# Low weight parts by accumulating DMA in a hybrid decoder layer (four gate/up blocks and all of down)

## The chip, the cores and the metric

The kernel runs on one core of one Trainium2 chip. The metric is the device time of one execution in microseconds (us). The engines named below are PE (matrix multiply; PEld is its weight load), ACT (ScalarE), DVE (VectorE), POOL (GpSimd) and SP (SyncE, which here only issues DMAs). Each engine works through its own queue in order; semaphores tie the queues together.

## What is computed

One decoder layer on 512 tokens of width 1024: a mixer with eight attention heads and eight gated groups, a projection back, a layer norm, then a SwiGLU feed-forward part with 2816 hidden units and a second layer norm.

```
merged = concat(rms_norm(attention(x @ w_q, x @ w_k, x @ w_v)), rms_norm(spatial_gating(gelu(x @ w_u), gelu(x @ w_z))))
x = layer_norm(alpha * x + merged @ w_out)             # "LN1" below
ffn = (silu(x @ w_gate) * (x @ w_up)) @ w_down
x = layer_norm(alpha * x + ffn)                        # "LN2"
```

All data are float32. The inputs weigh 58 MB as the chip reads them, nearly all of it weights.

## The kernel before, in words

**Split products.** PE multiplies in a float32 form that keeps fewer bits (F32R). To keep the accuracy, each operand is split into a high part (the operand rounded to F32R) and a low part (operand minus high part), and each product is three matmuls: high by high, high by low, low by high (`mm3`, and `product` in the gate/up stage). So every weight tile of 128 x 1024 (512 KB), after its load, needs a high copy and a low part. `split` (lines 232 to 241) makes them: the high copy on ACT (line 238), or on DVE for three tiles (line 236), and the low part by a subtraction (line 239) on DVE, or on POOL where the caller says so (`far`).

**Buffers.** The class `W` (line 251) holds a weight tile of q, k, z, u, out and down: the raw load `wr` rotates through 2 buffers, the high part `wh` and the low part `wl` through 3 each. A new tile can be split only when PE has finished with the tile three before it. Two early users have buffers of their own: the first four gate/up blocks (pairs 0 and 1; high parts `pth` and `ptl`, low parts `znh` and `znl`), and the last four tiles of down (`qk`, `qk`, `zg`, `ug`).

**Stages.** In the order of time: V and QK projections, attention mixed with the gated part, output projection of both halves, LN1 with its transposes, gate/up, down, LN2. Out-projection and LN1 go by four token tiles t = 0 to 3 of 128 tokens: two PSUM banks for each t (one for each half of the columns), then `layer_norm` (line 679): an add per half (line 750) that needs a reciprocal root `ra[t]` made on POOL (line 275, `pow`), statistics (687, 688), another pow on POOL, normalisation (700 on ACT or 696 and 707 on DVE), gain (702), bias (711; for t = 1 on POOL), then PE transposes (760) and the splits into operands of gate/up (`V`, `qk`, `xh`, `ug`).

**Gate/up.** Eleven pairs of hidden tiles; each pair takes seven block products instead of eight by a Strassen-like scheme, whose extra blocks are sums that DVE makes in PSUM (line 933). A block is 24 matmuls of 256 columns. For pairs 0 and 1 the first two blocks are prepared early, by `whole` (line 826), while out-projection and LN1 run.

**Down.** `down_w(f)` (line 963) loads and splits tile f of w_down and splits the hidden activations of that tile (ACT line 973, DVE line 974); `down_mm` multiplies for four token tiles and two halves, 24 matmuls of 512 columns a tile. 22 tiles; the last six are finished token tile by token tile, so that LN2 of a token tile runs beside the products of the next.

**What sets the order.** Every operation is recorded with an engine, a cost in us and the buffers that it reads and writes (`op`). `plan` (line 107) is a list scheduler: it simulates the engines with these costs, takes on each engine the ready operation of the lowest rank, and so fixes the order of every queue. The costs that concern the change are MM (one `mm3` on 512 columns), the cost of a DMA on SP and its latency DMA_LAT. A cost that is changed can move instructions on any engine, also far from the code it belongs to.

Of the kernel before, what the change touches and what calls it, by code (L numbers as in the profile page):

```python
# [8 lines left out]
AF = mybir.ActivationFunctionType  # L9
# [22 lines left out]

SAME, CROSS, DMA_LAT, MM, MM256 = 0.15, 0.19, 1.9, 0.643, 0.36
SEQ = ('q1', 'a1', 'q0', 'z', 'q2', 'a0', 'u', 'q3', 's', 'a2', 'a3')
# [27 lines left out]
class Order:  # L62
# [13 lines left out]

    def op(self, eng, cost, fn, r=(), w=(), base=None, table=None, lock=False):
        o = Op()
        o.eng, o.cost, o.fn, o.table, o.lock = eng, cost, fn, table, lock
        o.lat = DMA_LAT if eng == "SP" else 0.0  # L80
        o.prio = (self.base if base is None else base, len(self.ops))
# [104 lines left out]
def build(tc, cp, wp, ap, ps, xt, xtok, w_vqk, w_zu, w_out, w_gu, w_dn, wsp, cst, rows, cols, out):  # L186
# [5 lines left out]
    def act(n, fn, r, w, aps=0, acc=False, **k):  # L192
        od.op("ACT", 0.075 + 0.000833 * n + 0.093 * (aps + acc), fn, r, w, **k)
# [7 lines left out]
    def dma(kb, fn, r, w, **k):  # L201
        od.op("SP", max(0.46, kb / 352.0), fn, r, w, **k)
# [31 lines left out]
    def split(n, src, hi, lo, rs, ws_hi, ws_lo, far=False, lock=True, near=False, **k):  # L234
        if near:
            dve(n, lambda: V.tensor_scalar(hi(), src(), 1.0, None, op0=ALU.mult), rs, ws_hi, per=0.52, lock=True, **k)
        else:
# [3 lines left out]
               lock=lock, **k)  # L241

    def mm3(cost, o, lh, ll, rh, rl, start, stop, r, w, **k):
        def fn():
            PE.matmul(o(), lhsT=lh(), rhs=rh(), start=start, stop=False)  # L245
            PE.matmul(o(), lhsT=lh(), rhs=rl(), start=False, stop=False)  # L246
            PE.matmul(o(), lhsT=ll(), rhs=rh(), start=False, stop=stop)  # L247

        pe(cost, fn, r, w, **k)

    class W:


        def __init__(self, src, tag=None, mid=None, group=None):
# [12 lines left out]
            if mid is not None:  # L267
                mid(raw)
            split(WCH, lambda: raw.t, lambda: self.hi(every), lambda: self.lo(every), [raw], hk, lk, group in WPOOL,
                  near=group in WHI, base=RANK["w"])  # L270
# [525 lines left out]
    class Raw:  # L796


        def __init__(self, p, j, slot):
# [3 lines left out]
            else:  # L803
                self.t, self.key = (lambda c=slice(0, WCH): zgr.t[:, slot, c]), (zgr, slot)
            dma(512, lambda: nc.sync.dma_start(self.t(), w_gu[4 * p + j]), [], [self.key], base=PREP)

# [19 lines left out]
    def whole(raw, early=None):  # L826
        return Blk(early).fill(raw.t, raw.key, far=early in EPOOL)

# [78 lines left out]
    pairs = [Pair(p) for p in range(NP)]  # L907
    EARLY, EPOOL = 2, (0, 1, 2, 3)
    first = [[Raw(0, 0, "wr"), Raw(0, 3, "wr")], [Raw(1, 0, 0), Raw(1, 3, 1)]]
# [53 lines left out]
    def down_w(f, tag=None):  # L963
        w = W(w_dn[f], tag)
        if f < FT - 4:
# [112 lines left out]
```

## Time and profile before

| | us |
|---|---|
| three runs | 570.74, 571.74, 1094.83 |
| median of them | 571.74 |
| the profiled execution, its own time | 570.17 |
| its span in the trace | 568.1 |
| PE busy | 547.5 (96%) |
| DVE busy | 413.2 (73%) |
| ACT busy | 280.9 (49%) |
| POOL busy | 157.0 (28%) |
| DMA engines busy (queue q1) | 34.6% of 16 engines' span |

A busy PE is read with care: its instructions are pipelined, and an instruction that runs at half the clock counts as busy too. Besides the totals, these views are used: the windows (busy time of each engine and the granted clock of PE in a stretch), the waits (who waited for whom), the chain that ended last, and the timeline (instructions in order of time; the number in brackets behind a row is the idle time ahead of it and what ended it). A line number can be that of a helper: 239 stands for all subtractions of `split`.

### The profile page before, as it was taken

Reading aid. Unit: us, or ns where it says so; the run is one execution under the profiler, and the core shown is the slowest. Engines: PE = TensorE matmul, PEld = TensorE weight load, DVE = VectorE, ACT = ScalarE, POOL = GpSimd, SP = SyncE. Lnnn points to the kernel's source line nnn. Section 1 sums busy time; section 2 is a strip of 40 time slices with the busy share of each in tenths; the row PEclk is TensorE's granted clock in tenths of the full one; section 3 lists DMA queues with packets and bytes.
Section 4 is the critical chain, followed back from the end, with each engine's and each line's share of the span. In section 5 each row is a group of like instructions: output and inputs, shape, how many; then the busy total and the mean of one; then the engine's idle time right before and its main releaser. Section 6 shows DMA issues by size and latency. Waiting matters only on the chain.

```text
span 568.1 us, 8774 instructions
## 1 busy us (share of the span) xinstructions
PE 547.5 (96%) x3360; PEld 488.6 (86%) x3360; DVE 413.2 (73%) x707; ACT 280.9 (49%) x482; POOL 157.0 (28%) x119
## 2 busy tenths in 40 slices
PE   9999999999899968999999999999999999999994
PEld 5888888887688857999999999999999888888883
DVE  5537779879975699998788788888877723334385
ACT  6323796788864347544545544544455422323211
POOL 0026258613205730253333242343322200000011
PEclk9999999999999979899999999999999999999998
DMA  7745514155715201432332333333124332232311
GB/s 260 265 131 153 140 48 129 43 163 182 226 38 194 102 3 72 144 127 103 112 112 76 115 109 109 116 111 112 38 75 149 112 111 94 92 112 74 112 74 74
DMA packets 21225, 65.51 MB, mean 115 GB/s; under 512 B 2880, under 2 KB 3392, under 8 KB 21184
## 3 DMA queue, kind: packets, MB, share of 16 engines
q1 hardware_dynamic: 21184, 64.96, 34.6%
q8 instruction: 26, 0.43, 0.3%
q14 instruction: 15, 0.12, 0.1%
HBM read 58.66 MB, written 2.10 MB: 107 GB/s over the span
## 4 chain that ended last, share of the span: by engine, by line
PE 94%; DVE 2%; ACT 2%; issue 0%; POOL 0%; DVEq 0%
PE pj L838 22%; PE sc L838 17%; PE pj L245 12%; PE pj L247 12%; PE pj L246 12%; PE sc L245 2%; PE sc L247 2%; PE sc L246 2%; PE pv L481 2%; PE tp L464 1%; PE sc L426 1%; PE pv L247 1%; PE pv L245 1%; PE tp L247 1%; PE tp L245 1%; PE tp L246 1%
## 5 line engine op out<-in xcount | busy, mean ns | idle before, releaser
L239 DVE TENSOR_TENSOR wl<-wr,wh 128x1024 fp32r<-128x1024 f32 (+1 forms) x55 | 71.8, 1306 | 60.7 <-ACT wh L238 60.1
L238 ACT ACTIVATE wh<-wr 128x1024 fp32r<-128x1024 f32 (+1 forms) x58 | 57.8, 999 | 84.4 <-PE sc L247 54.0
L838 PE MATMUL pj<-qk,wh 128*128 128x256 f32 x352 | 65.6, 287 | 1.2 <-ACT wh L238 1.2
L838 PE MATMUL sc<-xh,wh 128*128 128x256 f32 x352 | 64.5, 284 | 0.0
L838 PEld LDWEIGHTS pj<-qk,wh 128*128 128x128 f32 x352 | 55.8, 195 | 1.4 <-ACT wh L238 1.4
L838 PEld LDWEIGHTS sc<-xh,wh 128*128 128x128 f32 x352 | 55.1, 193 | 0.0
L275 POOL TENSOR_TENSOR sm<-sm,only 128x1 f32<-128x1 f32 (+1 forms) x20 | 16.4, 825 | 137.8 <-DVE sm L274 137.7
L838 PE MATMUL pj<-V,wh 128*128 128x256 f32 x288 | 52.6, 283 | 0.0
L838 PE MATMUL pj<-qk,wl 128*128 128x256 f32 x176 | 50.7, 288 | 0.4 <-DVE wl L239 0.4
L838 PE MATMUL sc<-xh,wl 128*128 128x256 f32 x176 | 49.8, 283 | 0.0
L245 PE MATMUL pj<-wh,xh 128*128 128x512 f32 x114 | 46.3, 406 | 0.0
L838 PEld LDWEIGHTS pj<-V,wh 128*128 128x128 f32 x288 | 44.9, 192 | 0.0
L246 PE MATMUL pj<-wl,xh 128*128 128x512 f32 x114 | 44.6, 391 | 0.0
L838 PE MATMUL pj<-V,wl 128*128 128x256 f32 x144 | 40.8, 283 | 0.0
L247 PE MATMUL pj<-wh,xl 128*128 128x512 f32 x96 | 37.7, 393 | 0.0
L239 POOL TENSOR_TENSOR wl<-wr,wh 128x1024 fp32r<-128x1024 f32 x7 | 17.2, 2456 | 72.8 <-ACT wh L238 67.9
L838 PEld LDWEIGHTS pj<-qk,wl 128*128 128x128 f32 x176 | 34.3, 195 | 0.8 <-DVE wl L239 0.8
L838 PEld LDWEIGHTS sc<-xh,wl 128*128 128x128 f32 x176 | 33.9, 192 | 0.0
L238 ACT ACTIVATE wh<-tp 128x512 fp32r<-128x512 f32 x33 | 19.7, 596 | 27.9 <-PE sc L838 26.0
L838 PE MATMUL sc<-ug,wh 128*128 128x256 f32 x176 | 32.1, 283 | 0.0
L239 DVE TENSOR_TENSOR wl<-tp,wh 128x512 fp32r<-128x512 f32 x33 | 22.6, 684 | 8.6 <-ACT wh L238 8.6
L245 PE MATMUL pj<-wh,pr 128*128 128x512 f32 x72 | 28.0, 389 | 0.0
(331 smaller groups left out, 1512.1 us busy)
## 6 DMA issues: line engine op xcount, KB each, us to landing
wr<-w_dn SPq DMA_DIRECT2D x22, 512.0 KB, 3.2
zg<-w_gu SPq DMA_DIRECT2D x16, 512.0 KB, 3.4
wr<-w_gu SPq DMA_DIRECT2D x16, 512.0 KB, 3.5
kl<-w_gu SPq DMA_DIRECT2D x14, 512.0 KB, 3.3
wr<-w_vqk SPq DMA_DIRECT2D x8, 512.0 KB, 3.6
wr<-w_zu SPq DMA_DIRECT2D x8, 512.0 KB, 3.3
wr<-w_out SPq DMA_DIRECT2D x8, 512.0 KB, 4.1
wr<-w_vqk SPq DMA_DIRECT2D x8, 256.0 KB, 4.0
```

Source lines behind the costliest of these rows:

```text
L238: act(n, lambda: A.activation(hi(), src(), AF.Copy), rs, ws_hi, **k)
L239: either("P" if far else "D", n, lambda E: E.tensor_tensor(out=lo(), in0=src(), in1=hi().bitcast(F32), op=ALU.subtract), [*rs, *ws_hi], ws_lo,
L245: PE.matmul(o(), lhsT=lh(), rhs=rh(), start=start, stop=False)
L246: PE.matmul(o(), lhsT=lh(), rhs=rl(), start=False, stop=False)
L247: PE.matmul(o(), lhsT=ll(), rhs=rh(), start=False, stop=stop)
L275: od.op("POOL", 0.3 + 0.165 * n, lambda: PL.tensor_tensor(out=o.t, in0=v.t, in1=mhalf.t[:, :n], op=ALU.pow), [v, mhalf], [o], lock=True)
L426: PE.matmul(sc.t[:, :n], lhsT=qs.t[:, e, ts], rhs=ks.t[:, 2 * e + 1, :n], start=False, stop=True)
L464: PE.transpose(tp.t[:, j * P:j * P + P], p.t[:, j * P:j * P + P], ident.t)
L481: PE.matmul(pv.t[:, j * P:], lhsT=vs.t[:, j, h, :], rhs=pt.t[:, j * S:j * S + w], start=j == 0 and i == 0, stop=j == NT - 1 and i == 1)
L838: PE.matmul(o, lhsT=lh(w), rhs=buf.t[:, s + rh, x], start=first and side == k == i == 0, stop=k == 3 and i == 2, skip_group_check=True)
```

## The change

The low parts of the first four gate/up blocks and of all 22 tiles of down are no longer made by subtraction. ACT writes the high part, and then writes the tile with its sign turned, rounded to F32R, into the low part's place: that is minus the high part. Then a DMA issued from POOL's queue adds the weights once more from DRAM onto it, so that the operand minus the high part stands there. The raw tile is read by the two ACT copies alone. In the planner, one `mm3` costs 0.681 instead of 0.643, and an accumulating DMA takes POOL 1.0 and lands 4.0 later.

```
-SAME, CROSS, DMA_LAT, MM, MM256 = 0.15, 0.19, 1.9, 0.643, 0.36
+SAME, CROSS, DMA_LAT, MM, MM256 = 0.15, 0.19, 1.9, 0.681, 0.36
+GROW, GROW_LAT = 1.0, 4.0
...
-        o.lat = DMA_LAT if eng == "SP" else 0.0
+        o.lat = DMA_LAT if eng == "SP" else lat
...
+    def split_dram(n, src, dram, hi, lo, rs, ws_hi, ws_lo, **k):
+
+        act(n, lambda: A.activation(hi(), src(), AF.Copy), rs, ws_hi, **k)
+        act(n, lambda: A.activation(lo(), src(), AF.Copy, scale=-1.0), rs, ws_lo, **k)
+        od.op("POOL", GROW, lambda: nc.gpsimd.dma_start(lo(), dram, accum_op=ALU.add), ws_lo, ws_lo, lat=GROW_LAT, **k)
...
+            if group == "down":
+                split_dram(WCH, lambda: raw.t, src, lambda: self.hi(every), lambda: self.lo(every), [raw], hk, lk,
+                           base=RANK["w"])
+                return
...
     def whole(raw, early=None):
-        return Blk(early).fill(raw.t, raw.key, far=early in EPOOL)
+        if early is None:
+            return Blk(early).fill(raw.t, raw.key)
+        b, c = Blk(early), slice(0, WCH)
+        split_dram(WCH, raw.t, raw.src, lambda: b.hi(c), lambda: b.lo(c), [raw.key], [b.hk], [b.lk], base=PREP)
+        return b
...
-    EARLY, EPOOL = 2, (0, 1, 2, 3)
+    EARLY = 2
...
-        w = W(w_dn[f], tag)
+        w = W(w_dn[f], tag, group="down")
```

In the changed kernel the line numbers are 10 to 16 higher. Over the whole program DVE issues 22 instructions fewer, ACT 26 more, and POOL loses 4 subtractions and gets 26 DMAs; PE and SP issue the same instructions. Their order differs in many places before gate/up, hardly within gate/up, and little behind it.

**Place 1: POOL at the end of out-projection.** `sm` at L275 (L286 in the changed kernel) are the pow operations; the four in a row give `ra[t]`, the next ones the root of LN1's variance for t = 0 and t = 1; the rows on `znl` and `znh` are the low parts of the four early blocks. Before:

```order
L239 TENSOR_TENSOR znl_1997<-zg_1951,ptl_1986 128x1024
L239 TENSOR_TENSOR znl_1997<-zg_1951,ptl_2020 128x1024
L239 TENSOR_TENSOR znh_2049<-wr_1999,pth_2031 128x1024
L275 TENSOR_TENSOR sm_2077<-sm_2055,only_7_73 128x1
L275 TENSOR_TENSOR sm_2082<-sm_2060,only_7_73 128x1
L275 TENSOR_TENSOR sm_2088<-sm_2062,only_7_73 128x1
L275 TENSOR_TENSOR sm_2091<-sm_2064,only_7_73 128x1
L239 TENSOR_TENSOR znh_2049<-wr_2033,pth_2069 128x1024
L275 TENSOR_TENSOR sm_2125<-sm_2118,only_7_73 128x1
L275 TENSOR_TENSOR sm_2171<-sm_2160,only_7_73 128x1
```

Three of the four subtractions stand ahead of the first pow. In the changed kernel the same place reads:

```order
L286 TENSOR_TENSOR sm_2026<-sm_2018,only_7_73 128x1
L286 TENSOR_TENSOR sm_2034<-sm_2020,only_7_73 128x1
L286 TENSOR_TENSOR sm_2045<-sm_2022,only_7_73 128x1
L286 TENSOR_TENSOR sm_2051<-sm_2024,only_7_73 128x1
L248 DMA znl_2029<-w_gu 128x1024 x2
L248 DMA znh_2065<-w_gu 128x1024
L286 TENSOR_TENSOR sm_2102<-sm_2097,only_7_73 128x1
L248 DMA znh_2065<-w_gu 128x1024
L286 TENSOR_TENSOR sm_2123<-sm_2117,only_7_73 128x1
```

The four pows have moved ahead of everything that concerns the early blocks, and three of the accumulating DMAs stand ahead of the pow of t = 0, the fourth ahead of that of t = 1.

**Place 2: PE at the end of out-projection.** `tp` and `pv` at L760 (L771) are the transposes of a token tile's two halves, `pj_2114` is a bank of token tile 3, `pj_2227` the first early block's product. Before:

```order
L247 MATMUL pj_2107<-ug_2004,xh_1526 128x512
L245 MATMUL pj_2114<-ug_2004,xh_1526 128x512
L246 MATMUL pj_2114<-ug_2004,xh_1526 128x512
L247 MATMUL pj_2114<-ug_2004,xh_1526 128x512
L760 MATMUL tp_2155<-only_1_206,xl_1510 128x128 x4
L760 MATMUL pv_2164<-only_1_206,xl_1510 128x128 x4
L760 MATMUL tp_2197<-only_1_206,xl_1510 128x128 x4
L760 MATMUL pv_2213<-only_1_206,xl_1510 128x128 x4
L838 MATMUL pj_2227<-V_2174,pth_2031 128x256 x2
```

All of token tile 3's matmuls precede the transposes of t = 0 and t = 1. In the changed kernel, where `pj_2134` and `pj_2147` are token tile 3's banks:

```order
L254 MATMUL sc_2089<-ug_1997,xh_1516 128x512
L252 MATMUL pj_2134<-wh_1921,xh_1516 128x512
L253 MATMUL pj_2134<-wl_1930,xh_1516 128x512
L254 MATMUL pj_2134<-wh_1921,xh_1516 128x512
L771 MATMUL tp_2139<-only_1_206,xl_1555 128x128 x4
L252 MATMUL pj_2147<-wh_1921,xh_1516 128x512
L253 MATMUL pj_2147<-wl_1930,xh_1516 128x512
L254 MATMUL pj_2147<-wh_1921,xh_1516 128x512
L771 MATMUL pv_2153<-only_1_206,xl_1555 128x128 x4
L252 MATMUL pj_2134<-wh_1932,xh_1516 128x512
```

The transposes of t = 0 have moved 21 and 18 matmuls forward, into token tile 3's product. What these rows don't show: the banks of t = 0 are also finished sooner. Between the last matmul of its second bank and the first one of token tile 3 stand 18 matmuls of 512 columns before and 33 after the change, while the place of token tile 3's first matmul in PE's queue is the same.

**Place 3: ACT and POOL where gate/up ends.** `wh_4915` (`wh_4919`) is the high part of down's first tile, `pr` at L882 (L898) the silu of the last hidden tiles, `xh` and `pr` at L973 (L989) the splits of activations. ACT before:

```order
L238 ACTIVATE wh_4886<-wr_4506 128x1024
L238 ACTIVATE wh_4915<-wr_4813 128x1024
L882 ACTIVATE pr_4917<-pr_4917 128x256
L973 ACTIVATE xh_4950<-znh_4410 128x512
L973 ACTIVATE pr_4958<-atr_2366 128x512
L238 ACTIVATE wh_4963<-wr_4913 128x1024
```

and in the changed kernel:

```order
L239 ACTIVATE wh_4890<-wr_4510 128x1024
L246 ACTIVATE wh_4919<-wr_4817 128x1024
L898 ACTIVATE pr_4921<-pr_4921 128x256
L247 ACTIVATE wl_4933<-wr_4817 128x1024
L989 ACTIVATE pr_4945<-atr_2391 128x512
L989 ACTIVATE xh_4953<-znh_4414 128x512 x2
L246 ACTIVATE wh_4965<-wr_4917 128x1024
L247 ACTIVATE wl_4977<-wr_4917 128x1024
```

The negated copy `wl_4933` follows the high copy behind one short silu. POOL's queue there, in the changed kernel:

```order
L900 TENSOR_TENSOR znl_4892<-pr_4921 128x256
L248 DMA wl_4933<-w_dn 128x1024
L913 TENSOR_TENSOR pr_4963<-rt_4955,rt_4781 128x512
L248 DMA wl_4977<-w_dn 128x1024
L900 TENSOR_TENSOR znl_4892<-pr_4963 128x256
L248 DMA wl_5007<-w_dn 128x1024
L900 TENSOR_TENSOR znl_4892<-pr_5001 128x256
```

The accumulating DMAs of the first tiles stand between the last products of gate and up; on PE, down's first tile now begins behind both last blocks of gate/up, where six of its matmuls stood between these two before.

## Rows read from the trace of the kernel before

**Rows 1.** Windows: us; busy PE, PEld, DVE, ACT, POOL; PE's clock; DMA share; GB/s.
```profile
0.00:186.00 186.00, 182.00 (x886) 148.54 (x887) 138.77 (x327) 120.02 (x232) 64.56 (x48) 1.00 0.48 153
186.00:229.00 43.00, 34.09 (x200) 29.79 (x199) 36.35 (x73) 21.55 (x36) 14.36 (x13) 0.92 0.14 50
229.00:442.00 213.00, 213.00 (x1757) 212.52 (x1756) 178.93 (x227) 106.03 (x173) 72.64 (x54) 0.99 0.32 107
442.00:535.00 93.00, 93.00 (x412) 77.02 (x411) 36.11 (x41) 30.25 (x38) 2.34 (x2) 1.00 0.32 108
```

**Rows 2.** Waits of PE over the whole span: us in total, times, longest.
```profile
PE tp L760 <- POOL xl L711: 5.0, 1, 5.0
PE pj L838 <- ACT cs L860: 2.0, 1, 2.0
```

**Rows 3.** POOL's timeline, end of out-projection: start, duration, operation, [idle before].
```profile
188.25 2.40 POOL L239 TENSOR_TENSOR znh<-wr,pth 128x1024 fp32r<-128x1024 f32 x1
190.61 2.11 POOL L275 TENSOR_TENSOR sm<-sm,only 128x1 f32<-128x1 f32 x4
...
195.38 0.55 POOL L275 TENSOR_TENSOR sm<-sm,only 128x1 f32<-128x1 f32 x1 [0.29 <-DVE sm L274]
```

**Rows 4.** DVE's timeline, the same place and the end of LN1.
```profile
191.19 1.41 DVE L750 SCALAR_TENSOR_TENSOR xl<-pj,sm,xl 128x512 f32<-128x512 f32 x2 [3.46 <-POOL sm L275]
...
227.96 0.68 DVE L239 TENSOR_TENSOR wl<-tp,wh 128x512 fp32r<-128x512 f32 x1
```

**Rows 5.** PE's timeline: a bank of t = 0, t = 1's transposes, early blocks' ends.
```profile
189.84 0.39 PE L247 MATMUL pj<-ug,xh 128*128 128x512 f32 x1
190.07 0.39 PE L245 MATMUL pj<-ug,xh 128*128 128x512 f32 x1
...
206.27 1.11 PE L760 MATMUL tp<-only,xl 128*128 128x128 f32 x4 [4.96 <-POOL xl L711]
...
208.56 1.31 PE L838 MATMUL pj<-V,pth 128*128 128x256 f32 x2
...
226.27 0.28 PE L838 MATMUL pj<-V,znl 128*128 128x256 f32 x1
```

**Rows 6.** Windows of 2 us in LN1 and behind it, columns as in rows 1.
```profile
206.00:208.00 2.00, 1.62 (x7) 1.23 (x8) 1.90 (x5) 0.58 (x2) 2.00 (x4) 0.52 0.00 0
...
212.00:214.00 2.00, 2.00 (x15) 2.00 (x15) 2.00 (x4) 0.08 (x1) 0.00 (x0) 0.78 0.55 162
...
230.00:232.00 2.00, 2.00 (x10) 1.77 (x9) 2.00 (x4) 0.64 (x2) 1.71 (x1) 0.50 0.03 8
232.00:234.00 2.00, 2.00 (x14) 2.00 (x14) 1.93 (x4) 1.84 (x4) 0.00 (x0) 0.66 0.47 141
```

**Rows 7.** ACT's timeline, end of gate/up and two tiles of down.
```profile
434.81 1.06 ACT L238 ACTIVATE wh<-wr 128x1024 fp32r<-128x1024 f32 x1 [1.43 <-PE pj L838]
435.78 0.40 ACT L882 ACTIVATE pr<-pr 128x256 f32<-128x256 f32 x1
...
451.62 1.06 ACT L238 ACTIVATE wh<-wr 128x1024 fp32r<-128x1024 f32 x1 [3.79 <-PE sc L247]
...
457.06 1.06 ACT L238 ACTIVATE wh<-wr 128x1024 fp32r<-128x1024 f32 x1 [3.86 <-PE sc L247]
```

**Rows 8.** PE's timeline, last-but-one gate/up block and down's first matmul.
```profile
434.73 0.40 PE L838 MATMUL sc<-xh,wh 128*128 128x256 f32 x2
...
437.61 0.40 PE L245 MATMUL tp<-wh,pr 128*128 128x512 f32 x1
```

**Rows 9.** DMA: the queue (packets, MB, share of 16 engines), then down's loads.
```profile
q1 hardware_dynamic: 21184, 64.96, 34.6%
...
wr<-w_dn SPq DMA_DIRECT2D x22, 512.0 KB, 3.2
```

**Rows 10.** SP's timeline: one issue of a 512 KB load.
```profile
173.46 0.33 SPq L266 DMA_DIRECT2D wr<-w_out  x1
```

**Rows 11.** ACT's timeline, high parts of the early blocks.
```profile
185.52 1.04 ACT L238 ACTIVATE pth<-wr 128x1024 fp32r<-128x1024 f32 x1
```

More of the change, by code (lines that the diff above doesn't have):

```diff
@@ L75, in buf, with op @@
         return b
-    def op(self, eng, cost, fn, r=(), w=(), base=None, table=None, lock=False):
+    def op(self, eng, cost, fn, r=(), w=(), base=None, table=None, lock=False, lat=0.0):
         o = Op()
         o.eng, o.cost, o.fn, o.table, o.lock = eng, cost, fn, table, lock
-        o.lat = DMA_LAT if eng == "SP" else 0.0
+        o.lat = DMA_LAT if eng == "SP" else lat
         o.prio = (self.base if base is None else base, len(self.ops))
@@ L804, in __init__ @@
                 self.t, self.key = (lambda c=slice(0, WCH): zgr.t[:, slot, c]), (zgr, slot)
-            dma(512, lambda: nc.sync.dma_start(self.t(), w_gu[4 * p + j]), [], [self.key], base=PREP)
+            self.src = w_gu[4 * p + j]
+            dma(512, lambda: nc.sync.dma_start(self.t(), self.src), [], [self.key], base=PREP)
     class Blk:
```

## The prediction

> **What bounds the kernel now.** I read the windows by stage first [rows 1]. PE is busy 213.0 of 213.0 us in gate/up and 93.0 of 93.0 us in down, at a clock of 0.99 and 1.00: there only PE's own work counts, unless an operand comes late. Before 186 us it is busy 182 of 186. The one stage with room is the end of out-projection with LN1, 186 to 229 us: PE is busy 34.09 of 43 us and the clock is 0.92.
>
> The waits of PE tell where: the longest in the whole span is 5.0 us, on token tile 1's last LN1 operation on POOL; the next is 2.0 [rows 2]. PE is not the bound in this stage. DVE is: it is busy 36.35 of the 43 us [rows 1], and of the rest 3.46 are one wait ahead of its first LN1 add [rows 4]. So the chain of the stage starts with DVE's first LN1 add at 191.19 and goes on without a gap to speak of to the operand split at 227.96 [rows 4], behind which PE runs steadily.
>
> What the wait costs besides itself: after PE waited 4.96 us at 206.27 [rows 5], the windows show a granted clock of 0.52 from 206 us, and still 0.78 in 212 to 214 [rows 6]; 0.5 is the lower of the two levels, 1.2 instead of 2.4 GHz. I read a spell of 7.1 us (206.3 to 213.4). A second spell lies at 230 to 233.4 (0.50, then 0.66): about 3.4 us. While PE is the bound, half the clock loses half the spell. The first spell lies in a stretch where DVE is the bound and costs nothing; the second lies in steady gate/up and loses 1.7 us.
>
> **The change, step by step.** The sum is made against the profiled execution, 570.17 us, 1.57 below the median of 571.74.
>
> *(a) LN1 starts earlier: -4.2.* DVE's first add waits for the reciprocal roots on POOL. They stand behind subtractions, the last of which holds POOL from 188.25 to 190.61 [rows 3], although their inputs are ready when DVE falls idle, at 191.19-3.46 = 187.73 [rows 4]. The add's other input, the second bank, or half, of t = 0, is no hindrance for its first op: that op reads the first bank, whose last matmul ends at 189.84+0.39 = 190.23 [rows 5]. The add starts at 191.19, 0.96 later. In the changed kernel the pows stand first (Place 1), so the 0.96 goes. Further, the banks of t = 0 are finished 33 instead of 18 matmuls ahead of token tile 3 (Place 2): 15 matmuls at the spacing of 190.07-189.84 = 0.23, or 3.4 us. Less about 0.15 for the semaphore on the way: 0.96+3.4-0.15 = 4.2. DVE's operations behind the add are the same, so the stage's end should move by as much, to about 224.5. Bounds: 0.8 (the pows alone) and 4.8. The transposes of t = 0, stand earlier in PE's queue, but their data come sooner too; should they be late, token tile 3 is late with them, and DVE wants that last.
>
> *(b) PE's clock behind the stage: +1.8.* The wait of 4.96 us mostly goes, since t = 1 is ready earlier while PE's work ahead of its transposes is the same. PE then reaches the early blocks at about 203: 208.56 less the wait of 4.96 and some 0.6 that the transposes lost to the clock. The blocks with the transposes among them took 226.27+0.28-208.56 = 18.0 us [rows 5], of which 2.0 was the second wait of [rows 2] and 2.4 loss to the clock (half of 208.56 to 213.4), so 13.6 of work: done at 216.6. The operands of the next block come at about 224.5. So PE now idles some 8 us just ahead of the steady part. The row to go by is the 4.96 us wait, which was followed by 7.1 us at half clock; now this spell lies where PE is the bound and loses 3.5 instead of 1.7. Bounds: -1.7 (no spell: behind the wait of 2.0, at 221 to 223, the clock stayed) to +3.5.
>
> *(c) The passage to down: +2.3.* Before, ACT copies the high part at 434.81, and a subtraction follows on DVE. Now ACT copies (about 1.0), does the silu of 0.4 [rows 7] and copies with the sign turned, 436.2 to 437.2. Then POOL issues the accumulating DMA. The trace of before has none. Its issue is bounded by 0.33 (SP's issue of a load of the same size [rows 10]) and 2.40 (POOL's subtraction of such a tile [rows 3]); I take 1.0, nearer to the issue, since POOL writes no data. Its landing is bounded below by a plain load's 3.2 [rows 9]. One tile of 512 KB keeps the 16 engines busy for 0.346 x 568.1 x 0.5243/64.96 = 1.59 us [rows 9]; an addition must also fetch the destination, so I take 3.2+1.59 = 4.8, with three times 3.2 as the upper end. So the low part stands at 437.2+1.0+4.8 = 443.0. PE wants it in down's second matmul. Before, last blocks of gate/up and down's first tile were interleaved; now both blocks are done first (Place 3), each 437.61-434.73 = 2.88 us long [rows 8], so it is wanted at 434.73+2 x 2.88+0.23 = 440.7. PE waits 2.3 us. Bounds: 0.1 (0.33 and 3.2) to 8.5 (2.40 and 9.6). A wait of 2.3 is nearer to the 2.0 that kept the clock than to 4.96, so I add no spell.
>
> *(d) Down itself: 0.* One tile takes PE 457.06-451.62 = 5.44 us [rows 7]. High and low parts rotate through three buffers, so a tile may be made as soon as PE leaves the tile three before: two periods, 10.9 us, ahead of need. The new chain is two ACT copies of 1.06, 1.0 and 4.8, together 7.9. Cover: 3.0 us; it is gone if issue and landing exceed 8.8. Throughput: a tile now takes the DMA engines 1.59 for the raw load and, taken as two passes, 3.2 for the accumulation: 4.8 of 5.44 us. POOL does 2.34 us in 93 [rows 1], so 22 issues fit. ACT gets 26 copies of 1.06, all but four of them here, where it is busy 30 of 93 us; DVE saves 22 subtractions where it is busy 36 of 93 [rows 1]. Neither shortens anything while PE is full.
>
> *(e) The early low parts: 0.* Three of the DMAs stand ahead of t = 0's variance pow on POOL, the fourth ahead of t = 1's. That pow started 195.38-191.19 = 4.2 us after DVE's first add [rows 3, 4], which makes 191.2 from an add at 187.0. The third DMA needs ACT's negated copy of a tile whose high part began at 185.52 [rows 11]; ACT gets three copies of 1.0 more ahead of that copy's end, so the copy ends by 186.6+3.0 = 189.6. Cover: 1.6 us for the issue; I took 1.0. PE wants these low parts only behind the transposes.
>
> *(f) Elsewhere: 0, give or take 3.* The dearer `mm3` in the planner changes the order of every queue before LN1. PE has 4 us of room there in 186, which is what a better or worse order can be worth. LN2 behind down keeps its operations.
>
> Sum: 570.17-4.2+1.8+2.3 = 570.1.
>
> **The rivals.**
>
> *The accumulation fills the DMA engines (slower).* From 5.44-1.59 = 3.85 us of engine time per accumulated tile on, down is bound by DMA. If the destination's reading and writing are passes of their own, a tile costs three passes, 4.76, and with the load 6.35: 0.91 more than PE's period. Over the 18 tiles that use the ring this is 16.4 us: 586.6. For it: no row shows an addition in flight. Against it: reads and writes of the plain load go together in those 1.59, and a load's 3.2 are half latency.
>
> *No new spell and no wait at the passage (faster, but little).* If PE's clock holds as it is and the DMA lands in about 3.2 with a short issue, (b) and (c) are near 0: 570.17-4.2 = 566.0, at best 564 without the second spell. For it: DVE stays busy, PE's idle time may be split among several shorter waits, as that of 2.0 [rows 2]. Against it: PE's work in the stage is not changed, and with the wait in front gone the idle time collects behind it.
>
> *POOL is held at its DMAs.* If POOL takes as long for each early DMA as for the subtraction that it replaces, 2.4 us [rows 3], the change doesn't free POOL. The third DMA then ends at 189.6+2.4 = 192.0, 0.8 past the 191.2; the fourth, behind t = 0's pow, puts t = 1's pow about 1.8 later than DVE asks for it. Together 2.6: (a) keeps only 1.6 of 4.2, and 570.17-1.6+1.8+2.3 = 572.7; with a long wait at the passage as well, 577. For it: in LN1 DVE hardly pauses, and the price of 2.4 was paid beside it. Against it: a DMA's issue on SP takes 0.33 [rows 10]. The Trainium skill has such a rule (SBUF — State Buffer, section "SBUF: two separate sides"): POOL cannot write a DMA's descriptors while DVE runs an operation in a mode that takes the port that both share, a copy of float32 in SBUF for example. By that rule this rival is real where DVE is as full as in LN1; no run here shows such a case, and the DVE operations of LN1 are mostly of two inputs.
>
> **How the numbers follow.** Forecast .40, the sum with its own range of 566 to 574; no spell and no wait .26 (564 to 567); POOL held .19 (572 to 577); DMA-bound down .15 (582 upward). Two per cent is 11.4 us, about what a measurement of this kernel can tell from no change: faster means below 558.8 and slower above 581.6. Only an order before LN1 that fills PE's 4 us together with every favourable bound leads near 558.8: .04, out of the .26. The DMA-bound case holds the .15; the rest lies within, .81. The range leaves out little below the favourable case, 563.5, and the DMA-bound one above, 580.
>
> **What would show it.** (a): DVE's first LN1 add at about 187 instead of 191.2, the last split at about 223.8 instead of 227.96. (b): a wait of PE of 5 us or more ahead of steady gate/up and a clock near 0.5 for some 7 us behind it. (c): a wait of 1 to 4 us of PE at down's second matmul, ended by the accumulating queue. (d): PE busy at least 92 of 93 us in down, with a DMA share of some 0.85. (e): POOL's four DMA issues short, its pow for t = 0 not late. What would make it wrong first: waits of PE in every tile of down, on the accumulating queue; or LN1's chain starting where it did, since then (a) was not the pows and the banks.

## The result, and the profile after

The changed kernel takes 589.36 us, median of 4 (588.44 to 592.85), against 571.39 us before: a ratio of 1.033, 95% interval 1.0275 to 1.0385. It is slower by 18 us; the forecast was 570.1, within 563.5 to 580.0. The profiled execution has a span of 587.0 us, 18.9 more than before. One of the four runs of the kernel before took 1094.83 us and is left out of the ratio.

Windows by stage of the changed kernel, columns as in [rows 1]:

```profile
0.00:186.00 186.00, 176.91 (x855) 144.21 (x856) 134.40 (x323) 116.32 (x226) 63.02 (x45) 0.98 0.46 140
186.00:229.00 43.00, 37.30 (x226) 32.24 (x225) 37.85 (x71) 29.20 (x43) 14.82 (x15) 1.00 0.57 153
229.00:442.00 213.00, 208.05 (x1711) 207.45 (x1712) 177.68 (x228) 103.00 (x168) 70.35 (x51) 0.98 0.32 102
442.00:535.00 93.00, 88.41 (x403) 73.51 (x402) 18.18 (x24) 45.46 (x58) 18.60 (x21) 0.98 0.88 191
535.00:587.00 52.00, 39.36 (x170) 31.30 (x168) 21.39 (x42) 13.08 (x14) 7.77 (x9) 0.95 0.55 133
```

The borders stand at fixed times, and the stages have moved against them, so these rows tell where PE has new holes, not how long a stage is: 9.1 us ahead of 186 instead of 4.0, with some half clock (0.98 for 1.00), and new ones in the rows from 229 on. The longest waits of PE name them (us in total, times, longest):

```profile
PE pj L854 <- ACT wh L239: 6.0, 1, 6.0
PE tp L253 <- DMA wl<-w_dn: 3.6, 1, 3.6
PE pj L595 <- DVE ug L590: 2.7, 1, 2.7
PE pj L253 <- DMA wl<-w_dn: 2.4, 1, 2.4
PE tp L475 <- DVE sm L285: 2.1, 1, 2.1
```

The 5.0 of [rows 2] is gone, and 6.0 ahead of steady gate/up has come. Other waits are new too: for an accumulated low part of down (3.6 and 2.4, and 1.2 and 1.1 further down the list), and two ahead of LN1 (2.7, 2.1). Stage lengths, read off the timelines of both:

| | before | after | more |
|---|---|---|---|
| DVE's first LN1 add | 191.19 | 193.84 | 2.65 |
| PE starts steady gate/up | 228.69 | 232.30 | 3.6 |
| last gate/up matmul ends, less 1.38 for the six down matmuls that stood inside before | 440.65 | 448.29 | 7.6 |
| PE's last matmul ends | 560.38 | 579.09 | 18.7 |

So some 11 us were lost in down, and 7.6 ahead of it. Of these 7.6, steady gate/up itself lost 4.0, where the forecast had no term: 2.6 of them are three new waits of PE, the last just ahead of the last gate/up block:

```profile
445.18 0.48 PE L854 MATMUL sc<-ug,wh 128*128 128x256 f32 x2 [0.94 <-DVE rt L860]
```

### The profile page after: what moved, and what is told of

It is laid out like the page before. It is cut to its first block, busy times and chain, and to the rows that moved or that the text cites. A ratio compares the mean times of both kernels' runs of the same rounds, so it can differ in the third digit from the quotient of the medians.

```text
span 587.0 us, 8818 instructions
## 1 busy us (share of the span) xinstructions
PE 550.0 (94%) x3360; PEld 488.7 (83%) x3360; DVE 389.5 (66%) x685; ACT 307.1 (52%) x508; POOL 174.6 (30%) x141
## 4 chain that ended last, share of the span: by engine, by line
PE 68%; DMA 13%; DVE 11%; ACT 4%; issue 3%; SPq 1%; POOL 0%; DVEq 0%; ACTq 0%; POOLq 0%
PE pj L854 19%; PE sc L854 13%; PE pj L252 8%; PE pj L253 8%; PE pj L254 8%; DMA wr<-w_vqk 3%; DMA wr<-w_dn 2%; DVE wl L240 2%; DMA qk<-qk 2%; PE sc L254 2%; PE sc L252 2%; PE sc L253 2%; DMA wl<-w_dn 1%; PE tp L475 1%; DMA wr<-w_gu 1%
## 5 line engine op out<-in xcount | busy, mean ns | idle before, releaser
L240 DVE TENSOR_TENSOR wl<-wr,wh 128x1024 fp32r<-128x1024 f32 (+1 forms) x37 | 50.1, 1357 | 11.2 <-ACT wh L239 11.2
L239 ACT ACTIVATE wh<-wr 128x1024 fp32r<-128x1024 f32 (+1 forms) x40 | 38.7, 971 | 26.0 <-PE pj L253 9.9
L246 ACT ACTIVATE wh<-wr 128x1024 fp32r<-128x1024 f32 x18 | 19.1, 1060 | 48.2 <-PE sc L254 35.3
L248 POOL DMA_DIRECT2D wl<-w_dn x18 | 15.6, 867 | 76.0 <-ACT wl L247 76.0
L286 POOL TENSOR_TENSOR sm<-sm,only 128x1 f32<-128x1 f32 (+1 forms) x20 | 20.3, 1020 | 39.2 <-DVE sm L285 39.2
```

Source lines behind the costliest of these rows:

```text
L239: act(n, lambda: A.activation(hi(), src(), AF.Copy), rs, ws_hi, **k)
L240: either("P" if far else "D", n, lambda E: E.tensor_tensor(out=lo(), in0=src(), in1=hi().bitcast(F32), op=ALU.subtract), [*rs, *ws_hi], ws_lo,
L246: act(n, lambda: A.activation(hi(), src(), AF.Copy), rs, ws_hi, **k)
L248: od.op("POOL", GROW, lambda: nc.gpsimd.dma_start(lo(), dram, accum_op=ALU.add), ws_lo, ws_lo, lat=GROW_LAT, **k)
L286: od.op("POOL", 0.3 + 0.165 * n, lambda: PL.tensor_tensor(out=o.t, in0=v.t, in1=mhalf.t[:, :n], op=ALU.pow), [v, mhalf], [o], lock=True)
```

## The experiments

Each kernel is timed against the kernel before on its own chip (571.5 to 572.1 us there). In a label, m stands for the planner's number, e for the early blocks and d for down. Behind a time stand its lowest and highest run, behind a ratio its 95% interval. The cuts of code show the edit that matters, not always all of it.

**The three parts apart.** The change has three: the planner's number, the early blocks, down. `m_only`:

```
-SAME, CROSS, DMA_LAT, MM, MM256 = 0.15, 0.19, 1.9, 0.643, 0.36
+SAME, CROSS, DMA_LAT, MM, MM256 = 0.15, 0.19, 1.9, 0.681, 0.36
```

> The kernel before with one number of the planner changed, the cost of an mm3 (0.681 instead of 0.643); all low parts by subtraction. In the changed kernel DVE's first LN1 add came 2.65 us later than before (193.84 for 191.19), although the banks of t = 0 stand 15 matmuls earlier in PE's queue, and PE waited 7.7 us ahead of 160 us where it had waited 2.6. Theory order: the number alone does this through the order of the queues; the first add is late by 2 to 4 us, and the time is 573 to 577 us. Rival DMA: the order is worth nothing, and the late add comes from the early accumulating DMAs or the copies that they need; the time is 569 to 572 us.

Measured 579.96 us (576.0 to 583.67), ratio 1.0133 (1.0081 to 1.0184). The number alone loses 8 us, more than either theory said; the rival falls. But DVE's first add is not late in its trace (191.26). It waits for PE there, no longer for a pow: PE lost 4.1 us more than before on the way (2.6 in waits, 1.5 to half clock), and the earlier place of the banks made up for most of it. The loss lies behind the add. DVE, then POOL, at the same time:

```profile
196.41 2.34 DVE L691 SCALAR_TENSOR_TENSOR sm<-sm,sm 128x1 f32<-128x1 f32 x1
199.63 3.49 DVE L702 TENSOR_TENSOR xl<-xl,kl 128x512 f32<-128x512 f32 x2 [0.58 <-ACT xl L700]
```
```profile
196.33 2.40 POOL L239 TENSOR_TENSOR znh<-wr,pth 128x1024 fp32r<-128x1024 f32 x1
199.66 2.92 POOL L239 TENSOR_TENSOR znl<-zg,ptl 128x1024 fp32r<-128x1024 f32 x1
```

An operation on one column lasts 2.34 us, exactly until POOL's subtraction ends; in the kernel before the same line took 0.15:

```profile
196.34 0.15 DVE L691 SCALAR_TENSOR_TENSOR sm<-sm,sm 128x1 f32<-128x1 f32 x1
```

The number had put POOL's four early subtractions behind the pows, among LN1's operations. Two of them met DVE operations of two inputs, and each of these two held DVE for 2.2 us: 4.4 of the 4.6 us by which the way from the add to steady gate/up grew (42.1 for 37.5 us).

`d_only`, the changed kernel with 0.643 and with the early blocks as before (this cut shows the early blocks):

```
-        if early is None:
-            return Blk(early).fill(raw.t, raw.key)
-        b, c = Blk(early), slice(0, WCH)
-        split_dram(WCH, raw.t, raw.src, lambda: b.hi(c), lambda: b.lo(c), [raw.key], [b.hk], [b.lk], base=PREP)
-        return b
+        return Blk(early).fill(raw.t, raw.key, far=early in EPOOL)
```

> Down's low parts by accumulating DMA; the early blocks by subtraction on POOL and the planner's number 0.643 as in the kernel before. Theory ends of down: 11 of the 19 us of the changed kernel were lost at down's two ends (waits of PE for an accumulated low part of 3.65 us at the first tile and of 2.44, 1.11 and 1.17 us at the last six tiles, and half clock behind them), none in its middle, where ACT's copies kept a period of 5.44 us; so the time is 579 to 583 us, with the same waits. Rival order: the passage was lost because 0.681 put both last blocks of gate/up ahead of down's first tile; with 0.643 the wait at the first tile is below 1.5 us or its clock spell is gone, and the time is 573 to 577 us.

Measured 583.72, ratio 1.0199 (1.0181 to 1.0217): 11.6 us. The rival falls: the old number doesn't mend the passage. PE's four waits for accumulated parts:

```profile
446.10 0.80 PE L253 MATMUL tp<-wl,pr 128*128 128x512 f32 x1 [2.62 <-DMA wl<-w_dn]
...
539.81 0.50 PE L253 MATMUL pj<-wl,pr 128*128 128x512 f32 x1 [2.07 <-DMA wl<-w_dn]
...
543.14 0.50 PE L253 MATMUL pj<-qk,xh 128*128 128x512 f32 x1 [0.98 <-DMA qk<-w_dn]
...
550.86 0.50 PE L253 MATMUL pj<-zg,xh 128*128 128x512 f32 x1 [1.30 <-DMA zg<-w_dn]
```

One stands at the first tile and three at the last six; between 446 and 539 there is none.

`e_only`, the early blocks alone, again with 0.643:

```
-        w = W(w_dn[f], tag, group="down")
+        w = W(w_dn[f], tag)
```

> The first four gate/up blocks' low parts by accumulating DMA; down by subtraction and 0.643 as in the kernel before. Theory ACT: in the changed kernel t = 0's normalisation stood on ACT behind two copies of the fourth early tile, whose raw load came 7.4 us after its issue while the accumulating DMAs kept the DMA engines full; DVE waited 2.83 us for it. Without the late order ahead of it, the add comes at about 187 to 190, the wait on ACT stays, and the time is 569 to 573 us. Rival clock: what counts is only the wait of 6 us of PE ahead of steady gate/up and the half clock behind it (about 2 to 3 us more than before); 572 to 575 us. Rival of my prediction's sum without its clock term: 566 us.

Measured 568.45, ratio 0.9929 (0.9906 to 0.9952): faster than the kernel before, a little under the theory's 569 to 573. DVE, POOL and PE of this kernel:

```profile
189.86 1.41 DVE L761 SCALAR_TENSOR_TENSOR xl<-pj,sm,xl 128x512 f32<-128x512 f32 x2 [0.54 <-POOL sm L286]
...
197.22 0.16 DVE L702 SCALAR_TENSOR_TENSOR sm<-sm,sm 128x1 f32<-128x1 f32 x1 [2.13 <-POOL sm L286]
```
```profile
195.74 0.86 POOL L248 DMA_DIRECT2D znh<-w_gu  x1 [2.69 <-ACT znh L247]
196.31 0.88 POOL L286 TENSOR_TENSOR sm<-sm,only 128x1 f32<-128x1 f32 x1
```
```profile
228.23 0.39 PE L854 MATMUL pj<-qk,wl 128*128 128x256 f32 x1 [4.05 <-DVE wl L240]
```

DVE's wait ahead of the first add fell from 3.46 [rows 4] to 0.54. Then 2.13 is given back: t = 0's pow stands behind the fourth accumulating DMA, which waits for ACT's copy of a late raw tile. The wait was on POOL, not on ACT as the theory had it. The profiled executions of the two kernels are only 0.75 us apart (569.42 and 570.17; the first is the slowest of its four), so these rows show where something was gained and lost, and not how the 3.6 us of the medians come about.

`ed` is the changed kernel with 0.643:

> The changed kernel with the planner's number put back to 0.643: both parts by accumulating DMA. If the three parts add up (order, early blocks, down), the time is that of the changed kernel less what the number alone costs, 582 to 586 us of 589.4. If the number matters only together with the accumulating DMAs (at the passage to down), 577 to 582 us.

Measured 582.61 (577.9 to 584.49), ratio 1.0168 (1.0111 to 1.0225). The parts add up roughly: 572.1+11.6-3.6 = 580.1, and 2.5 more were measured. Its trace has them in down, where PE's waits for accumulated parts come to 9.26 us, against 6.97 in `d_only`; why they are longer beside the early blocks stays open. `me`, the combination that was missing (0.681 and the early blocks):

> The missing combination: the planner's 0.681 and the early blocks by accumulating DMA, down by subtraction. In m_only (580.0 us, 7.9 over the kernel before) POOL's four subtractions of the early blocks moved among LN1's operations, and beside each of them a DVE operation of two inputs from the buffer memory lasted 2.2 us longer than elsewhere (a 128x1 one 2.34 instead of 0.15, a pair of gains 3.49 instead of 1.28). Theory hold: the accumulating DMAs take those subtractions away, DVE isn't held there, and the time is 575 to 578 us. Rival order: what 0.681 costs is the order ahead of and in LN1 itself, which the DMAs don't mend: 579 to 582 us. By the sum of what was measured (589.4 less d_only's 11.6) it would be 577.8.

Measured 574.59, ratio 1.0079 (1.0047 to 1.0111): 5.4 us under `m_only`. The rival falls, and the hold is gone with the subtractions. The number still costs 6 us against `e_only`, of which the two profiled executions show 4.1. PE waits 2.80, 1.95 and 1.28 us at 147, 144 and 57 us (0.27, 0.99 and none in `e_only`), and the clock is at its lower level from 145.4 to 152.2, so that the first add comes 3.1 later. LN1 makes up for 1.9 of it, and steady gate/up, behind a wait of 6.04 in place of 4.05, takes 2.4 longer.

**Where down loses.** Three kernels, each `d_only` with a condition on the tile:

```
-        w = W(w_dn[f], tag, group="down")
+        w = W(w_dn[f], tag, group="down" if f > 2 else None)                   # d_nofirst
+        w = W(w_dn[f], tag, group="down" if f < FT - TAIL else None)           # d_notail
+        w = W(w_dn[f], tag, group="down" if 2 < f < FT - TAIL else None)       # d_mid
```

> Only down by accumulating DMA, as in d_only (583.7 us, 11.6 over the kernel before), but its first three tiles are split by subtraction on DVE; early blocks and planner as in the kernel before. Theory ends: the wait of PE at down's second matmul (2.62 us in d_only) and the half clock behind it, and with the old interleaving of the last gate/up blocks, come to 4 to 6 us: 577 to 580 us, the waits at the last six tiles stay. Rival DMA load: the loss comes from the DMA engines being nearly full throughout, the wait moves on to the fourth tile, and the time stays at 582 to 584 us.

Measured 580.10 (576.86 to 582.27), ratio 1.0149 (1.0106 to 1.0191): 3.6 us less than `d_only`. The waits at the last six tiles stay (4.35 in sum), and the one at the first tile is gone.

> Only down by accumulating DMA, as in d_only, but the last six tiles, those that are finished token tile by token tile, are split by subtraction. Theory ends: the waits of 2.07, 0.98 and 1.30 us there go, and what LN2 loses behind them: 4 to 6 us less than d_only, 577 to 580 us, with the wait at the first tile unchanged. Rival DMA load: the ring itself runs out, so that the waits move to the tiles ahead of the last six: 581 to 584 us.

Measured 577.57 (573.37 to 578.34), ratio 1.0096 (1.0067 to 1.0125): 6.1 us less, with 2.56 of waiting left at the first tile.

> Both of the last two edits: accumulating DMAs for tiles 3 to 15 of down alone. Theory ends: in the middle the accumulated low part comes some 10 us behind the slot's release, within the ring's 10.9, and PE doesn't wait: 571 to 573 us, the time of the kernel before, though 13 of 22 tiles are accumulated. Rival DMA load: 574 us or more, with waits of PE on accumulated tiles in the middle.

Measured 571.85 (570.17 to 574.65), ratio 1.001 (0.9991 to 1.003). All of down's loss is at its ends, and 13 accumulated tiles in the middle are free. PE's waits in `d_mid`, the two longest and the one for an accumulated part:

```profile
PE tp L771 <- POOL xl L722: 5.0, 1, 5.0
PE pj L850 <- ACT cs L872: 2.0, 1, 2.0
...
PE tp L253 <- DMA wl<-w_dn: 0.2, 1, 0.2
```

**Why the landing is long.** `d_halfload` leaves out every second raw load:

```
+            if load:
+                dma(512, lambda: nc.sync.dma_start(raw.t, src), [], [raw], base=RANK["w"])
...
+        w = W(w_dn[f], tag, group="down", raw=raws.pop() if f % 2 else None)
```

> d_only with the raw loads of every second tile of down left out: the copies of an odd tile read the raw tile before it, so the output is not the reference's there. The accumulating DMAs are all made. Theory contention: the median landing of an accumulation, 7.7 us in d_only, is long because a raw load runs beside it (1.6 us of the engines' time each); it falls to 6 or less, and the waits of PE at both ends of down become shorter by 1 us or more in all. Rival: an accumulation takes that long by itself, two passes one after the other with their own latencies: 7 to 8 us as before.

Measured 577.93 (two runs). The median landing of the 18 tiles in the rotating buffers fell from 7.7 to 6.6 us, not quite to 6; PE's waits for accumulated parts fell from 6.97 to 3.76 in sum (1.01 at the first tile, 2.75 at the end). So the load beside it is part of it, but not all: the last two tiles landed later than in `d_only` (6.9 and 7.5 us for 5.8 and 6.9), and an odd tile's copies no longer wait for a load of their own, which shortens waits by itself. The DMA issues of the changed kernel say the same (KB each, median us to landing):

```profile
q0 software_dynamic: 3744, 13.63, 13.3%
...
wr<-w_dn SPq DMA_DIRECT2D x22, 512.0 KB, 5.5
wl<-w_dn POOLq DMA_DIRECT2D x18, 512.0 KB, 7.8
...
znl<-w_gu POOLq DMA_DIRECT2D x2, 512.0 KB, 10.5
znh<-w_gu POOLq DMA_DIRECT2D x2, 512.0 KB, 10.6
...
zg<-w_dn POOLq DMA_DIRECT2D x1, 512.0 KB, 5.2
```

10.5 where several raw loads and accumulations are under way together, 7.8 with one load beside it, 5.2 near the end, where the raw loads run out. The raw loads pay too: 5.5 instead of 3.2 [rows 9]. Part of a landing passes before anything moves: by the packet records of the traces, the first packet follows its issue by 2.1 us at down's first tile (`d_only`) and by 4.5 us at the first early block of the changed kernel (at 198.17). What holds it there is not shown.

**LN1's start.** `pow_first` is the kernel before with one more edge in the planner:

```
-        return Blk(early).fill(raw.t, raw.key, far=early in EPOOL)
+        return Blk(early).fill(raw.t, raw.key, far=early in EPOOL, after=[ra[3]] if early == 0 else ())
```

> The kernel before with one edge more in the planner: the low part of the first early tile, a subtraction on POOL, waits for the root ra of token tile 3. So the four pows stand ahead of two of the subtractions instead of one; nothing is accumulated. My prediction's step (a) alone: DVE's first add starts about 2.9 us earlier (the roots' inputs are there at 187.73 and one pow takes 0.53), and the time falls to 568 to 569.5 us. Theory hold: the two subtractions, 4.8 us on POOL, now run beside LN1's first operations and ahead of t = 0's pow, DVE is held or waits for that pow, and the gain is given back: 571 to 575 us.

Measured 573.25, ratio 1.003 (1.0016 to 1.0045). The second theory's number is right, but not for its reason: no operation of DVE was held beside the two subtractions, and t = 0's pow was not waited for. DVE's wait ahead of the first add:

```profile
192.89 1.41 DVE L750 SCALAR_TENSOR_TENSOR xl<-pj,sm,xl 128x512 f32<-128x512 f32 x2 [2.62 <-POOL sm L275]
```

2.62 instead of 3.46: moving the pows alone shortens the wait by 0.84, near the 0.96 of step (a). Yet the add comes 1.70 later than before in this execution, since PE was later ahead of it (6.1 us of idle time instead of 4.0), and the way from it to steady gate/up is 2.4 us longer (39.9): PE waits 5.58 instead of 4.96 at the transposes of t = 1, and 3.12 ahead of steady gate/up.

`e_lat` tells the planner that the early raw loads land later:

```
+        o.lat = DMA_LAT + lat if eng == "SP" else lat
...
+    first = [[Raw(0, 0, "wr", 3.5), Raw(0, 3, "wr", 3.5)], [Raw(1, 0, 0, 3.5), Raw(1, 3, 1, 3.5)]]
```

> Only the early blocks by accumulating DMA, as in e_only (568.5 us), with one more number in the planner: the raw loads of the four early tiles land 3.5 us later in its reckoning. In e_only the roots for t = 0 stood on POOL behind the fourth accumulating DMA, that one waited for ACT's copies, and these for a raw load that landed late; DVE waited 2.13 us. Here the pows of t = 0 and t = 1 stand ahead of the fourth DMA. Theory queue: DVE's wait goes and the time is 565.5 to 567.5 us. Rival: DVE's chain is 2 us shorter but PE then idles as long ahead of steady gate/up, or loses it to half clock: 568 to 570 us.

Measured 568.07, ratio 0.9928 (0.9905 to 0.995). The rival is right: the wait for POOL is gone and DVE's way from the first add to steady gate/up is 2.0 us shorter than in `e_only` (36.4 for 38.4), but PE still waits 3.56 us for the first low part of steady gate/up, and the clock is at the lower level behind that.

`e_dmid` joins `e_only` with the condition of `d_mid`:

> The parts of the change that cost nothing, together: early blocks and tiles 3 to 15 of down by accumulating DMA, the other tiles of down by subtraction, planner as before. If the parts are independent, the time is that of e_only, 567 to 570 us (faster than both kernels); if the middle of down costs something that d_mid hid, 572 or more.

Measured 569.07, ratio 0.9957 (0.994 to 0.9975), as if independent. `e_only` and `e_lat` beat both kernels of the study.

## Why the prediction was wrong

By the parts, the sum that should have been written is 8 for the planner's number, 11.6 for down and -3.6 for the early blocks: 16 of the 18 us measured. The prediction had 0, +2.3 and -2.4. So three of its steps failed: (f) and (d), taken as 0, and (c), taken too small; (a) was taken too large. That the 16 come so near is partly luck, since the parts act on each other: 4.4 of the 8 are a hold that the changed kernel doesn't have, the number costs 6 to 7 beside the other parts all the same, and PE's waits for accumulated parts are 8.37 in the changed kernel, not 6.97.

**(f), the order: taken as 0 give or take 3, measured 8 alone and 6 to 7 beside the other parts (`me` less `e_only`, the changed kernel less `ed`).** The bound was PE's idle time ahead of LN1, the 4 us that an order could fill. It left out that a new order can make PE wait where it did not, with half the clock behind it, and that it can put two engines beside each other that hold one another. In the changed kernel the first of these counts. Its first add waits for PE, whose last matmul for it ends at 193.73 (190.23 before):

```profile
193.34 0.39 PE L254 MATMUL pj<-ug,xh 128*128 128x512 f32 x1
```
```profile
193.84 1.41 DVE L761 SCALAR_TENSOR_TENSOR xl<-pj,sm,xl 128x512 f32<-128x512 f32 x2 [2.10 <-PE pj L254]
```

PE runs without a gap from 160 to there (busy 33.00 of 33.00 us from 160 to 193); it was late before that. The windows around its two new waits, before, and then after:

```profile
144.00:152.00 8.00, 6.71 (x35) 5.21 (x36) 7.58 (x15) 7.15 (x15) 2.09 (x3) 1.00 0.87 298
```
```profile
144.00:152.00 8.00, 5.12 (x17) 3.77 (x18) 6.80 (x14) 7.10 (x14) 3.79 (x3) 0.57 0.98 323
```

PE idles 5.1 us more ahead of 160, and of the spell at the lower clock level, 144.8 to 151.6, it works 4.4 us at half speed and loses 2.2. Against these 7.3 the banks stand 3.4 earlier in the queue, so the bank should come 3.9 later, and comes 3.5 later. That is why the add comes 2.65 later instead of 4.2 sooner, although it no longer waits for a pow behind its bank. `me` shows the same two waits and a spell of the same length; `ed`, with the old number, has no wait above 1.1 us and no spell there.

DVE is also held once ahead of LN1, by POOL's subtraction for an out-projection tile (186.90 to 189.68):

```profile
187.36 2.87 DVE L669 SCALAR_TENSOR_TENSOR xh<-atr,only,xh 128x512 fp32r<-128x512 f32 x1
```

This line took 0.75 in the kernel before. It is not what made the add late: `m_only` has the same 2.87 and an add that is on time, and DVE was idle for 2.10 ahead of the add. Holds of this kind cost time in LN1 of `m_only`. The order in POOL's queue was shown in front of me, and I priced only who waits there, not who runs beside it.

**(a): right in kind, too large.** DVE's wait ahead of the add went from 3.46 to 0.54 in `e_only`, so 2.9 was to be had, and not 4.2; the add itself came 1.33 sooner (189.86). The rows said so: inputs at 187.73 and one pow of 0.53 give 188.3, and the sum put the add at 187.0. The input that then comes last counts; I added the gains of two of them and didn't hold the sum against the third.

**(e): the wrong queue.** The cover was worked out for POOL's issue. The issue was indeed short (0.86 to 1.55 us, where 1.0 was taken), in LN1 as well, so the rival in which POOL is held fell, and with it the rule of the Trainium skill on descriptors (SBUF — State Buffer, section "SBUF: two separate sides") had no price in the issues here; whether it has one in the long landings, no run shows. What was late is the raw load of the fourth early tile. ACT and DVE in the changed kernel:

```profile
199.61 1.06 ACT L246 ACTIVATE pth<-wr 128x1024 fp32r<-128x1024 f32 x1 [3.96 <-DMA wr<-w_gu]
...
201.52 1.50 ACT L711 ACTIVATE xl<-xl,sm,sm 128x512 f32<-128x512 f32 x2
```
```profile
202.35 1.40 DVE L713 TENSOR_TENSOR xl<-xl,kl 128x512 f32<-128x512 f32 x2 [2.83 <-ACT xl L711]
```

The load was issued at 192.25 and took until 199.5. Three more raw loads were issued between 189.70 and 193.71, and three accumulations from 193.65 on; the first packet of an accumulation is at 198.17, so by the packet records only raw loads moved until then, and what made this one long is not settled. The normalisation of t = 0 stands behind its two copies on ACT, and DVE, the bound of this stage, waits 2.83 us. In `me`, with the same queues, it waited 0.86, so this size goes with when the load lands.

**(b): right in kind, too large.** PE idles 6.03 us ahead of steady gate/up, and the clock is low behind it:

```profile
230.00:232.00 2.00, 0.00 (x0) 0.00 (x0) 2.00 (x5) 0.48 (x2) 0.00 (x0) 0.53 0.00 0
232.00:234.00 2.00, 1.70 (x6) 1.47 (x7) 1.94 (x4) 0.85 (x2) 1.70 (x1) 0.50 0.00 0
234.00:236.00 2.00, 2.00 (x12) 2.00 (x11) 1.94 (x4) 1.19 (x2) 0.67 (x1) 0.50 0.08 27
236.00:238.00 2.00, 2.00 (x15) 2.00 (x15) 1.33 (x3) 0.32 (x1) 0.00 (x0) 0.76 0.74 244
```

The spell is 6.8 us long, but the clock fell at about 230, while PE was idle: PE loses 0.85+1.0+0.48 = 2.3 us, against 1.7 before. The term was +1.8 and is +0.6.

**(c): +2.3, measured 3.6 in time (`d_only` less `d_nofirst`), and 4.3 in the trace of `d_only`, 2.6 of waiting and 1.7 lost to the clock.** The issue took 0.86 for 1.0, the landing 7.8 for 4.8: it was reckoned as a transfer by itself, and SP's raw loads for the next tiles run at that very place. And the wait of 2.62 had half the clock behind it (0.53 and 0.62 in the windows from 446 to 450, some 1.7 us lost), where I had judged 2.3 nearer to the wait that kept it. Beside this stands the 0.94 ahead of the last gate/up block: it is there in `d_only`, `d_notail`, `d_halfload`, `ed` and the changed kernel, which accumulate the first tile, and in none of the others, so it goes with giving up the interleaving of the last blocks (Place 3), for which the sum had no price. The 3.6 of the times says less than the trace, since `d_nofirst` is 2.1 later than `d_only` at the first LN1 add already.

**(d): 0, measured 0 in the middle and 6.1 at the end.** The middle went as worked out: two passes, 0.133 x 587.0/26 = 3.0 us of engine time per accumulation (3.2 taken), DMA share 0.88 (0.85 forecast). Copies, issue and landing come to some 10.1 us of the 10.9 that the three rotating buffers allow, where 7.9 was taken. So the slower rival, whose 586.6 lies near the measured time, is wrong too: three passes would have shown in the middle. What I left out is that the last six tiles are finished token tile by token tile, so PE wants all six within a few us, and a steady 5.44 per tile is no measure there. ACT's high copies for the four tiles with buffers of their own, before, and then after:

```profile
523.31 1.04 ACT L238 ACTIVATE qk<-wr 128x1024 fp32r<-128x1024 f32 x1
527.91 1.06 ACT L238 ACTIVATE qk<-wr 128x1024 fp32r<-128x1024 f32 x1 [3.56 <-DMA wr<-w_dn]
530.23 1.06 ACT L238 ACTIVATE zg<-wr 128x1024 fp32r<-128x1024 f32 x1 [1.26 <-DMA wr<-w_dn]
533.67 1.06 ACT L238 ACTIVATE ug<-wr 128x1024 fp32r<-128x1024 f32 x1 [2.38 <-DMA wr<-w_dn]
```
```profile
537.74 1.06 ACT L246 ACTIVATE qk<-wr 128x1024 fp32r<-128x1024 f32 x1 [0.27 <-DMA wr<-w_dn]
...
542.91 1.06 ACT L246 ACTIVATE qk<-wr 128x1024 fp32r<-128x1024 f32 x1 [3.16 <-DMA wr<-w_dn]
...
548.29 1.06 ACT L246 ACTIVATE zg<-wr 128x1024 fp32r<-128x1024 f32 x1 [3.38 <-DMA wr<-w_dn]
...
551.36 1.06 ACT L246 ACTIVATE ug<-wr 128x1024 fp32r<-128x1024 f32 x1 [1.06 <-DMA wr<-w_dn]
```

Before, the four came within 10.4 us, paced by loads alone; after, within 13.6, and each then still needs its accumulation, which lands 5.2 to 8.9 us behind its issue. In this stretch (534 to 554) the DMA engines are busy 0.97 of the time, against 0.92 from 470 to 520, where PE doesn't wait. That the DMA engines are the bound at the end is argued from these rows; `d_halfload`, with half the raw loads, still waited 2.75 there, against 4.35 in `d_only`.

What stays open: why the four executions of `m_only` spread from 576.0 to 583.7 us. Its trace has a span 6.0 us over that of the kernel before, and what the others lost beyond that isn't seen.

## What to carry to other kernels

A transfer that is covered in the steady part of a rotation of buffers must be priced again at both ends: where the buffers fill, beside the first loads, and where the consumer takes the last tiles faster than one per period. When a planner's number changes with the code, time it alone; here it cost 6 to 8 of the 18 us, by new waits of PE well ahead of the changed code, by the clock behind them and, alone, by which engines came to run beside each other. And when several inputs release an operation, gains of single inputs don't add up: its new start is set by the input that then comes last.

## What the hardware showed beyond that

- A POOL subtraction of two tiles in the buffer memory and a DVE operation with two inputs there exclude each other: 0.15 became 2.34 us and a pair of 1.28 became 3.49, each until POOL was done. Statistics of one input and adds that take one input from PSUM ran beside such a subtraction at their usual 1.28 and 0.7 (`pow_first`, 192.8 to 197.6). The Trainium skill tells of this (SBUF — State Buffer, section "SBUF: two separate sides": the pair of ports that both share is locked for a whole instruction), and these rows agree. A DMA issue on POOL never lasted above 1.55 us in LN1, nor did it hold DVE.
- An accumulating DMA of 512 KB costs the engines 3.0 us, where a plain load costs 1.6 (worked out as in the prediction), and lands in 5.2 to 10.6 us (medians by tile). A raw load beside it is part of that (`d_halfload`).
- The clock doesn't follow the length of PE's last wait alone. Behind 2.62 us at down's first tile it was 0.53; behind 2.44 at the last tiles of the changed kernel it stayed at 1.00; behind 1.01 (`d_halfload`) at 1.00, and behind 2.75 in that kernel at 0.50.
